# w_out by two-by-two blocks with seven products in an encoder block on one core

## The chip, the cores and the metric

The kernel runs on one core of a Trainium2 chip. The metric is the device time of one execution in microseconds (us), the median of several runs. The engines are named as in the profile: PE (TensorE matmul), PEld (its weight load), DVE (VectorE), ACT (ScalarE), POOL (GpSimd), SP (SyncE, which issues most transfers).

## What is computed

One layer of an encoder on a stream of 16 meta tokens and 1024 frames, width 1024, all float32: a half-step SwiGLU feed-forward, a mixing part (window attention and gated linear attention, GLA), a second half-step feed-forward, a final norm. The part that matters here, from the reference:

```python
    mixed = (jax.nn.sigmoid(gate_a) * (ya @ w_branch_att[l])
             + jax.nn.sigmoid(gate_b) * (yb @ w_branch_gla[l]))
    h = h + mixed @ w_out[l]
    h = h + 0.5 * swiglu(rmsnorm(h, ffn2_norm[l]), ffn2_w_gate[l], ffn2_w_up[l], ffn2_w_down[l])
```

`mixed` is 1024 wide, `w_out` is 1024 x 1024. Only the 1024 frames go through this part.

## The kernel before

**Number format.** Each float32 matrix is cut into a high and a low half in fp32r (`hi = cast(x)` on ACT, `lo = x - hi` on DVE), and each product of two 128-wide tiles is three matmuls: hi x hi, hi x lo, lo x hi. Tokens lie along the free axis, features along the 128 partitions, so a matmul of 512 columns is 128 features by 512 tokens.

**The feed-forwards** already multiply by blocks: `Seven` splits weights and tokens two by two and makes seven block products of the eight, with sums of weight blocks (S1 to S4) and of token blocks (T1 to T4). Their order and accumulators are in `PRODUCTS`; `Group.sums` makes S1 to S4 and `halves` makes the cuts. Their matmuls are line 464, their weight cuts lines 229 and 230, the weight sums line 447, the reading of a bank in the down projection line 344.

**The branch products** (`branch_units`): `ya @ w_branch_att` was multiplied by its gate and stored in `gates`; then `yb @ w_branch_gla` runs in 16 units (8 feature tiles m, 2 token halves). `load_b` fetches both gates' tiles, `ev_b` multiplies the bank (`br`) by the sigmoid (line 1584), adds the stored half (line 1585), and splits the result into `mx_` (lines 101, 102), tiles `mh` and `ml`.

**w_out** comes next: for each token half c and each of the 8 feature tiles m, a weight tile of 128 columns is fetched (512 KB) and cut (lines 125, 126), so each weight is fetched and cut twice. One bank `wo` takes 24 matmuls (8 k x 3, lines 96 to 98). DVE adds the residual `hm`, which was fetched from `h_dram` (line 1646), ACT squares it, and POOL, near the end DVE, adds the squares into `acc` (line 1657). `scales_total` sums `acc` over features with four small matmuls (`tot`) and takes the root, `scales_spread` turns the result into rows, and `rescale` (line 1623) makes the normed tokens, which are cut to be the second feed-forward's operands.

**After it** the feed-forward's last two feature tiles (`HEADS`) are done plainly, eight products' worth at a time (`plain`, banks `pg` and `pu`); then the token sums and the seven-product loop (`gate_ups`, `down`).

**Order of the work.** A scheduler orders each engine's instructions by priority and readiness, except inside `manual_schedule`, where the engines named keep the order in which the code is written. w_out stands outside such a piece. A tile pool (`tile_pool`) gives its memory back when it is closed; whoever takes the same place next waits until its last reader is done. [...]

```python
    for c in range(2):
        ...
        for m in range(KT):
            wh, wl = ktiles(wt.cut(wt.raw(cols_view(w_out, m * P))))
            hm = ub[c][m] = block("hm")
            nc.sync.dma_start(out=hm, in_=h_dram[m, :, c * HALF:(c + 1) * HALF])
            ps = bank("wo")
            cols = slice(c * HALF, (c + 1) * HALF)
            mm(ps, wh, wl, [t[:, cols] for t in mx_[0]], [t[:, cols] for t in mx_[1]])
            ...
            nc.vector.tensor_add(hm, ps, hm)
```

Of the kernel before, what the change touches and what calls it, by code (L numbers as in the profile page):

```python
# [8 lines left out]
F32 = mybir.dt.float32  # L9
# [8 lines left out]
P = 128  # L18
# [17 lines left out]
def hybrid_kernel(  # L36
# [25 lines left out]
    def ttile(name, dt=F32, n=512):  # L62
        return tmp.tile([P, TW], dt, tag="t", name=name)[:, 0:n]
# [1463 lines left out]
    def out_gate(i, chunks):  # L1527

        for c0, n in chunks:
            a, g = ttile("a"), ttile("g")  # L1530
            nc.sync.dma_start(out=a, in_=gr_dram[i, :, c0:c0 + n])
            nc.scalar.activation(g, a, AF.Sigmoid)
            nc.vector.tensor_mul(a, a, g)
            pt = bank("ot")
            o = heads[i // 2].o[i % 2]
            for t in range(4):
                nc.tensor.transpose(pt[:, t * P:(t + 1) * P], o[:, c0 + t * P:c0 + (t + 1) * P], ident)
            nc.vector.scalar_tensor_tensor(a, pt, vec[:, GO:GO + 1], a, op0=ALU.mult, op1=ALU.mult)
            split(yb[0][i][:, c0:c0 + n], yb[1][i][:, c0:c0 + n], a)
# [25 lines left out]
        fill.pop(0)()  # L1565
    for i in range(4):
        out_gate(i, CH_FR[1:2])
    right.close()


    mx_ = [[atile(f"m{hl}{i}", F32R) for i in range(KT)] for hl in "hl"]

    def load_b(m, c0, n):
        l = []
        for i in (8 + m, m):
            g = gtile("gl") if i < 8 else ttile("gl")
            nc.sync.dma_start(out=g[:, 0:n], in_=gates[i, :, c0:c0 + n])
            l.append(g)
        return l

    def ev_b(ps, m, c0, n, l):
        gb, a = l[0][:, 0:n], l[1][:, 0:n]
        nc.scalar.activation(gb, gb, AF.Sigmoid)
        nc.vector.tensor_mul(gb, ps[:, 0:n], gb)
# [4 lines left out]
    for u in units[0][0:2] + units[1][0:2] + units[0][2:4] + units[1][2:4] + units[2] + units[3]:  # L1589
        u()  # L1590
    gla.close()

    HALF = 512
    right = ctx.enter_context(ExitStack())
    t_a = right.enter_context(tc.tile_pool(name="ta", bufs=8, side="right"))
    blk = right.enter_context(tc.tile_pool(name="blk", bufs=17, side="right"))
    pools = [t_a, None, blk, None, w_main]  # L1600
    h2_dram = dram.tile([2, KT, P, HALF], F32, name="h2_dram")

    def scales_total(acc):
        ps = bank("tot")
# [17 lines left out]
        u = ub[c][m]  # L1622
        nc.vector.scalar_tensor_tensor(u, u, vec[:, G2 + m:G2 + m + 1], accs[c], op0=ALU.mult, op1=ALU.mult)

    def acc2(kind, which, turn):
        return bank(f"p{kind}")

    ffn2 = Seven("f2", HALF, acc2, pools, ffn2_w_gate, ffn2_w_up, ffn2_w_down)
    tops, block = ffn2.tops, ffn2.block
    ub = [[None] * KT, [None] * KT]  # L1630
    accs = []
    for c in range(2):
        acc = ttile(f"acc{c}")
        accs.append(acc)
        for m in range(KT):
            wh, wl = ktiles(wt.cut(wt.raw(cols_view(w_out, m * P))))
            hm = ub[c][m] = block("hm")
            nc.sync.dma_start(out=hm, in_=h_dram[m, :, c * HALF:(c + 1) * HALF])
            ps = bank("wo")
            cols = slice(c * HALF, (c + 1) * HALF)  # L1640
            mm(ps, wh, wl, [t[:, cols] for t in mx_[0]], [t[:, cols] for t in mx_[1]])
            if c == 1 and m == 0:
                first_dg = scales_total(accs[0])
            if c == 1 and m == 1:
                scales_spread(accs[0], first_dg)
            nc.vector.tensor_add(hm, ps, hm)
            if c == 1 and m >= 1:
                for k in (range(2) if m == 1 else [m] if m < KT else []):
                    rescale(k, 0)
                    tops["B11" if k < 4 else "B21"][k % 4] = ffn2.halves(ffn2.operand(True, "tb"), ub[0][k])  # L1650
            nc.sync.dma_start(out=h2_dram[c, m], in_=hm)
            if m == 0:
                nc.scalar.activation(acc, hm, AF.Square)
            else:
                sq = ttile("sq")
                nc.scalar.activation(sq, hm, AF.Square)
                (nc.vector if m >= KT - 2 else nc.gpsimd).tensor_add(acc, acc, sq)
# [6 lines left out]
    ffn2.w_ext = f2.enter_context(tc.tile_pool(name="wext2", bufs=2))  # L1664
    ffn2.s_pool = f2.enter_context(tc.tile_pool(name="sums", bufs=4))
    ffn2.ring = [w_main] * 6 + [ffn2.w_ext] * 2


    heads = [[ffn2.plain_weights(cols_view(w, f * P)) for w in (ffn2_w_gate, ffn2_w_up)] for f in HEADS]
    out_c = [[None] * 2 for _ in range(2)]  # L1670

    def plain(f, c, between=()):
        ts = [tops["B11"] + tops["B21"], tops["B12"] + tops["B22"]][c]
        pss = []
        for i in range(2):
            ps = bank("pg" if i == 0 else "pu")
            pss.append(ps)
            mm(ps, *ktiles(heads[f][i]), [x[:, 0:HALF] for x in ts], [x[:, HALF:] for x in ts])
            if between:
                between[i]()  # L1680
        g = ttile("g0")
        nc.scalar.activation(g, pss[0], AF.Silu)
        out_c[f][c] = block("m0")
        nc.vector.tensor_mul(out_c[f][c], pss[1], g)

    state = {}

    def second():
        state["dg"] = scales_total(accs[1])

    def third():
        scales_spread(accs[1], state["dg"])
        for m in range(KT):
            rescale(m, 1)
            tops["B12" if m < 4 else "B22"][m % 4] = ffn2.halves(ffn2.operand(False, "tb"), ub[1][m])
# [98 lines left out]
```

## Time and profile before

| what | value |
|---|---|
| median of 3 runs | 1999.52 us (1994.55 to 1999.86) |
| span of the profiled execution | 1994.6 us |
| granted TensorE clock, mean | 0.999 |
| PE busy | 1976.3 us, 99% |
| DVE, ACT, POOL busy | 1402.4, 897.2, 166.9 us |
| GLA branch products on PE | about 1210 to 1253 us |
| w_out on PE | about 1253 to 1342 us |
| plain gate/up and start of the loop | from 1342 us |

The profiled execution's own time is its span, within 0.1 us of the fastest of the three runs and 4.9 us below their median. In the profile's rows a group is line, engine, operation, out<-in, shape and count, then busy us and mean ns of one, then idle time before it and what ended it. In the time line a row is start, length, engine, line and operation.

### The profile page before, as it was taken

How to read it: one execution, taken by the hardware profiler on the slowest of the kernel's cores; microseconds unless marked ns; L12 is line 12 of the kernel's file. 1: busy time of each engine (PE TensorE's matmuls, PEld its weight loads, DVE VectorE, ACT ScalarE, POOL GpSimd, SP SyncE). 2: the span in 40 equal slices, each digit the busy share in tenths (PEclk: the TensorE clock that was granted, in tenths of full speed). 3: DMA queues.
4: the chain of work that ended last, by engine and by line, in shares of the span. 5: the costliest groups of instructions: out<-in, count | busy, mean ns of one | idle time of the engine just before them, and what ended most of it. 6: DMA issues, size and time to landing. Idle time of an engine off the chain costs nothing. (4 is left out here: it accounts for less than half of the span.)

```text
span 1994.6 us, 31746 instructions
## 1 busy us (share of the span) xinstructions
PE 1976.3 (99%) x11964; PEld 1755.8 (88%) x11964; DVE 1402.4 (70%) x2455; ACT 897.2 (45%) x1756; POOL 166.9 (8%) x196
## 2 busy tenths in 40 slices
PE   8999999999999999999999999999999999999998
PEld 8999999999999988888888778888888888888887
DVE  6976776677678785476466568568767766767886
ACT  5544444444322254465366545345444544442225
POOL 1000000001222000004100000110000000022220
PEclk9999999999999999999999999999999999999999
DMA  6343454348875333355212647742434543589722
GB/s 214 108 150 126 146 180 137 118 150 322 271 283 194 96 124 109 110 184 176 53 54 70 205 151 218 249 139 79 160 127 137 187 142 127 190 300 328 282 102 85
DMA packets 279721, 328.23 MB, mean 165 GB/s; under 512 B 25734, under 2 KB 191360, under 8 KB 279568
## 3 DMA queue, kind: packets, MB, share of 16 engines
q1 hardware_dynamic: 263936, 272.20, 41.5%
q10 hardware_dynamic: 15280, 53.89, 7.5%
q8 instruction: 94, 1.54, 0.3%
q14 instruction: 59, 0.48, 0.1%
q0 software_dynamic: 352, 0.11, 0.1%
HBM read 213.26 MB, written 112.88 MB: 164 GB/s over the span
## 5 line engine op out<-in xcount | busy, mean ns | idle before, releaser
L464 PE MATMUL pb<-tt,wop 128*128 128x260 f32 (+1 forms) x2280 | 393.0, 326 | 0.0
L464 PEld LDWEIGHTS pb<-tt,wop 128*128 128x128 f32 x2280 | 339.7, 188 | 35.5
L229 ACT CAST wop<-s 128x512 fp32r<-128x512 f32 x268 | 166.1, 621 | 236.9 <-PE pb L464 102.9
L230 DVE TENSOR_TENSOR wop<-s,wop 128x512 fp32r<-128x512 f32 x268 | 187.9, 704 | 114.8 <-ACT wop L229 114.3
L464 PE MATMUL pb<-tm,wop 128*128 128x260 f32 (+1 forms) x1440 | 233.7, 318 | 0.0
L229 ACT CAST wop<-raw 128x512 fp32r<-128x512 f32 x201 | 124.8, 621 | 225.4 <-PE pb L464 114.7
L464 PEld LDWEIGHTS pb<-tm,wop 128*128 128x128 f32 x1440 | 207.0, 188 | 18.7
L230 DVE TENSOR_TENSOR wop<-raw,wop 128x512 fp32r<-128x512 f32 x201 | 140.0, 697 | 34.3 <-ACT wop L229 34.2
L464 PE MATMUL pd<-tt,wop 128*128 128x260 f32 (+1 forms) x792 | 138.2, 327 | 0.0
L464 PEld LDWEIGHTS pd<-tt,wop 128*128 128x128 f32 x792 | 118.8, 188 | 13.1
L447 POOL TENSOR_TENSOR s<-raw 128x512 f32<-128x512 f32 x28 | 37.4, 1336 | 1025.0 <-DVE wop L230 538.8
L344 DVE SCALAR_TENSOR_TENSOR h<-pb,h 128x520 f32<-128x520 f32 (+1 forms) x136 | 94.0, 693 | 37.3 <-PE pb L464 35.4
L464 PE MATMUL pd<-tm,wop 128*128 128x260 f32 (+1 forms) x720 | 118.8, 319 | 0.0
L464 PE MATMUL pb<-tb,wop 128*128 128x260 f32 (+1 forms) x696 | 115.3, 319 | 0.7 <-DVE m L752 0.7
L464 PE MATMUL pd<-tb,wop 128*128 128x260 f32 (+1 forms) x696 | 115.1, 319 | 0.0
L464 PE MATMUL pa<-tb,wop 128*128 128x260 f32 (+1 forms) x696 | 115.0, 318 | 0.0
L464 PEld LDWEIGHTS pd<-tm,wop 128*128 128x128 f32 x720 | 104.2, 188 | 9.4
L464 PEld LDWEIGHTS pb<-tb,wop 128*128 128x128 f32 x696 | 100.9, 188 | 10.2 <-ACT vec L87 0.8
L464 PEld LDWEIGHTS pa<-tb,wop 128*128 128x128 f32 x696 | 100.7, 188 | 9.4
L464 PEld LDWEIGHTS pd<-tb,wop 128*128 128x128 f32 x696 | 100.7, 188 | 9.4
L447 DVE TENSOR_TENSOR s<-raw 128x512 f32<-128x512 f32 x92 | 63.3, 688 | 54.5 <-DMA raw<-in_ffn_w_up 50.6
L96 PE MATMUL pj<-uh,whi 128*128 128x512 f32 (+2 forms) x256 | 91.5, 357 | 0.0
(417 smaller groups left out, 3880.2 us busy)
## 6 DMA issues: line engine op xcount, KB each, us to landing
tm<-f1mid ACTq DMA_DIRECT2D x49, 520.0 KB, 5.4
tm<-f2mid ACTq DMA_DIRECT2D x49, 512.0 KB, 4.6
raw<-in_ffn_w_gate SPq DMA_DIRECT2D x42, 512.0 KB, 3.9
raw<-in_ffn_w_up SPq DMA_DIRECT2D x42, 512.0 KB, 3.9
raw<-in_ffn_w_down SPq DMA_DIRECT2D x80, 256.0 KB, 5.1
f1mid<-kh SPq DMA_DIRECT2D x63, 260.0 KB, 2.7
f1mid<-kl SPq DMA_DIRECT2D x63, 260.0 KB, 2.8
f2mid<-kh SPq DMA_DIRECT2D x63, 256.0 KB, 2.8
```

The costliest lines, as they stand in the source:

```text
L96: nc.tensor.matmul(ps, wh[k], xh[k], start=(k == 0), stop=False)
L229: nc.scalar.copy(x[:, 0:n], src)
L230: nc.vector.tensor_sub(x[:, n:2 * n], src, x[:, 0:n].bitcast(F32))
L344: nc.vector.scalar_tensor_tensor(hm, ps, 0.5, hm, op0=ALU.mult, op1=ALU.add)
L447: (eng.tensor_add if add else eng.tensor_sub)(a[s], a[x], a[y])
L464: nc.tensor.matmul(ps, y, z[:, s0:s0 + sn], start=(first and k == 0 and at == 0), stop=(at == 2 and k == len(cols) - 1), skip_group_check= ...
```

## The change

w_out becomes seven block products as in the feed-forward. Weights are four 512 x 512 blocks: A11 and A12 for the first 512 output features (first and second 512 input features), A21 and A22 for the rest. Tokens are B11, B21 (input features 0 to 511 and 512 to 1023 of the first token half), B12, B22 (second half). `ev_b` keeps the mixed tokens as raw float32 (`raw11`, `mixed`) and cuts B11, B21 and B22 (not B12) into operands `mx`. Each of the seven steps runs over four k-tiles; for each of the 28 pairs (i, k) four banks take three matmuls each. Weights are cut by `weights_of`, three pairs ahead; four kinds of bank group are used: b (steps 0, 2, 3, 4, one group, accumulating), a (step 1), d (steps 5, 6).

The residual is added in the reading of a bank: `started` adds the bank to the fetched residual, `finished` with a bank adds a second bank to it, `finished` without one stores the sum and squares it. A bank group b is read after step 0 (in the middle of step 1), after step 2, after step 3 and after step 4.

Weight sums and T4 go to POOL, T1 to T3 to DVE; the low halves of T1's cuts, of the `HEADS` weights (`head_weights`) and of five of the eight first operands (`first_tops`) go to POOL. The whole piece up to the end of the first `plain` is inside `manual_schedule` for ACT, DVE and PE; POOL and SP are ordered by the scheduler. `plain` runs gate and up side by side over k, with the second half's total (`second`) after k = 4. A21 and A22 lie in a pool (`ta`) that is opened when the branch's operands (`yb`) are done with.

```diff
+    raw11 = mix.enter_context(tc.tile_pool(name="raw11", bufs=4))
+    yb_pool = ybs.enter_context(tc.tile_pool(name="yb", bufs=8))
...
+    STEPS = (("b", "A11", "B11"), ("a", "A12", "B21"), ("b", "S2", "T2"), ("b", "S3", "T3"), ("b", "A22", "T4"),
+             ("d", "S1", "T1"), ("d", "S4", "B22"))
+    def weights_of(i, k):
+        w, a = ffn2.ring_tile("wop"), wa[STEPS[i][1], k]
+        cut_w[i, k] = w
+        nc.scalar.copy(w[:, 0:WB], a)
+        nc.vector.tensor_sub(w[:, WB:], a, w[:, 0:WB].bitcast(F32))
+    def cut_operand(name, k, src, eng=None):
+        x = wtop[name, k] = opd("mx")
+        nc.scalar.copy(x[:, 0:HALF], src)
+        (eng or nc.vector).tensor_sub(x[:, HALF:2 * HALF], src, x[:, 0:HALF].bitcast(F32))
...
-        split(mx_[0][m][:, c0:c0 + n], mx_[1][m][:, c0:c0 + n], a)
+        name, k = f"B{m // 4 + 1}{c0 // HALF + 1}", m % 4
+        mixed[name, k] = a
+        if name != "B12":
+            cut_operand(name, k, a)
...
+    ybs.close()
+    t_a = right.enter_context(tc.tile_pool(name="ta", bufs=8, side="right"))
...
+    def weight_sums(k):
+        s1 = wa["S1", k] = s1_tiles[k // 2][:, (k % 2) * WB:(k % 2 + 1) * WB]
+        nc.gpsimd.tensor_add(s1, wa["A21", k], wa["A22", k])
+        wa["S3", k] = wa["A21", k]
+        nc.gpsimd.tensor_sub(wa["S3", k], wa["A11", k], wa["A21", k])
+        wa["S2", k] = wa["A11", k]
+        nc.gpsimd.tensor_sub(wa["S2", k], s1, wa["A11", k])
+    def t_sum(name, k):
+        x, y = {"T1": ("B12", "B11"), "T3": ("B22", "B12"), "T2": ("B22", "T1"), "T4": ("B21", "T2")}[name]
+        to = {"T1": "B11", "T3": "B12", "T2": "B22", "T4": "B21"}[name]
+        (nc.gpsimd if name == "T4" else nc.vector).tensor_sub(mixed[to, k], mixed[x, k], mixed[y, k])
...
+    for k in range(4):
+        work[0, k] += [lambda k=k: weight_sums(k)]
+        work[3, k] += [lambda k=k: last_weight_sum(k)]
...
+    for n, (i, k) in enumerate(steps):
+        kind, _, name = STEPS[i]
+        if n + AHEAD < len(steps):
+            weights_of(*steps[n + AHEAD])
+        fresh = kind not in banks
+        if fresh:
+            banks[kind] = [bank(f"p{kind}") for _ in range(4)]
+        w, x = cut_w.pop((i, k)), wtop[name, k]
+        for j in range(4):
+            wh, wl = w[:, j * P:(j + 1) * P], w[:, WB + j * P:WB + (j + 1) * P]
+            for at, (y, z) in enumerate(((wh, x[:, 0:HALF]), (wh, x[:, HALF:2 * HALF]), (wl, x[:, 0:HALF]))):
+                nc.tensor.matmul(banks[kind][j], y, z, start=(fresh and k == 0 and at == 0), stop=(at == 2 and k == 3),
+                                 skip_group_check=True)
+        for go in work[i, k]:
+            go()
+        while waiting and (i, k) in ((1, 0), (2, 0)):
+            waiting.pop(0)()
...
+                elif i == 2:
+                    started(1, j, ps)
...
+    plain(0, 0, {0: lambda: head_weights(1, 0, (w_main, w_main)), 4: second, 5: lambda: head_weights(1, 1, (w_main, w_main)), 7: third})
```

What stands in the engines' own orders. On POOL, before, the only work of the w_out stretch are the additions of squares, up to the gate/up loop's weight sums (`acc` is the running sum, `sq` one tile's squares):

```order
L1657 TENSOR_TENSOR acc0_14128<-acc0_14128,sq_14200 128x512
L1657 TENSOR_TENSOR acc0_14128<-acc0_14128,sq_14238 128x512
L1657 TENSOR_TENSOR acc0_14128<-acc0_14128,sq_14276 128x512
L1657 TENSOR_TENSOR acc0_14128<-acc0_14128,sq_14314 128x512
L1657 TENSOR_TENSOR acc0_14128<-acc0_14128,sq_14352 128x512
```

On POOL, now, from the same place (line 1702 makes S1, 1704 S3, 1706 S2, 1710 S4, 1715 T4; `wa2` holds A21 or A22, `wa11` A11, `wa12` A12):

```order
L1715 TENSOR_TENSOR mixed_13949<-mixed_13949,mixed_13995 128x512
L1702 TENSOR_TENSOR s1_14159<-wa2_14147 128x512
L1702 TENSOR_TENSOR s1_14159<-wa2_14150 128x512
L1704 TENSOR_TENSOR wa2_14147<-wa11_13743,wa2_14147 128x512
L1704 TENSOR_TENSOR wa2_14150<-wa11_13743,wa2_14150 128x512
L1706 TENSOR_TENSOR wa11_13743<-s1_14159,wa11_13743 128x512 x2
L1702 TENSOR_TENSOR s1_14160<-wa2_14153 128x512
L1715 TENSOR_TENSOR mixed_13972<-mixed_13972,mixed_14018 128x512
L1704 TENSOR_TENSOR wa2_14153<-wa11_13744,wa2_14153 128x512
L1702 TENSOR_TENSOR s1_14160<-wa2_14156 128x512
L1706 TENSOR_TENSOR wa11_13744<-s1_14160,wa11_13744 128x512
L1704 TENSOR_TENSOR wa2_14156<-wa11_13744,wa2_14156 128x512
```

Thirteen sums stand here where additions of squares stood; S4 of the first k and S2 of the last come next, then three more S4 and two T4 before the first addition of squares.

On DVE, before, at the end of the branch and the start of w_out (`ml` is a low half of mixed tokens, `wlo` of a weight tile, `hm` the residual):

```order
L102 TENSOR_TENSOR ml6_13740<-gl_14076,mh6_13732 128x512
L1584 TENSOR_TENSOR gl_14096<-br_14100,gl_14096 128x512
L1585 TENSOR_TENSOR gl_14098<-gl_14098,gl_14096 128x512
L126 TENSOR_TENSOR wlo_14206<-raw_14203,whi_14205 128x1024
L102 TENSOR_TENSOR ml7_13741<-gl_14098,mh7_13733 128x512
L126 TENSOR_TENSOR wlo_14244<-raw_14241,whi_14243 128x1024
L1646 TENSOR_TENSOR hm_14135<-wo_14137,hm_14135 128x512
L1646 TENSOR_TENSOR hm_14171<-wo_14173,hm_14171 128x512
```

On DVE, now, from the first cut of a T2 operand (line 1615) over weight cuts (1602) and token sums (1715) to the first reading of a bank (1683):

```order
L1615 TENSOR_TENSOR mx_14206<-mixed_13995,mx_14206 128x512
L1602 TENSOR_TENSOR wop_14212<-wa12_13751,wop_14212 128x512
L1715 TENSOR_TENSOR r11_13788<-mixed_13883,r11_13788 128x512
L1715 TENSOR_TENSOR mixed_13883<-mixed_14018,mixed_13883 128x512
L1715 TENSOR_TENSOR mixed_14018<-mixed_14018,r11_13788 128x512
L1602 TENSOR_TENSOR wop_14233<-wa12_13753,wop_14233 128x512
L1615 TENSOR_TENSOR mx_14248<-mixed_14018,mx_14248 128x512
L1602 TENSOR_TENSOR wop_14254<-wa12_13755,wop_14254 128x512
L1715 TENSOR_TENSOR r11_13817<-mixed_13903,r11_13817 128x512
L1715 TENSOR_TENSOR mixed_13903<-mixed_14099,mixed_13903 128x512
L1715 TENSOR_TENSOR mixed_14099<-mixed_14099,r11_13817 128x512
L1683 TENSOR_TENSOR hm_14276<-pb_14169,hm_14276 128x512
```

Where the first reading of a bank followed the last weight cut directly, eleven cuts and sums of two SBUF tiles now stand ahead of it.

More of the change, by code (lines that the diff above doesn't have):

```diff
@@ L1567, in hybrid_kernel @@
         out_gate(i, CH_FR[1:2])
+    gla.close()
     right.close()
-    mx_ = [[atile(f"m{hl}{i}", F32R) for i in range(KT)] for hl in "hl"]
-    def load_b(m, c0, n):
[L1574 to L1579, printed above, removed]
+    HALF = 512
+    right = ctx.enter_context(ExitStack())
+    blk = right.enter_context(tc.tile_pool(name="blk", bufs=17, side="right"))
@@ new lines, in hybrid_kernel, with acc2 @@
+    w_ext = right.enter_context(tc.tile_pool(name="wext2", bufs=2, side="right"))
+    s_pool = right.enter_context(tc.tile_pool(name="sums2", bufs=4, side="right"))
+    h2_dram = dram.tile([2, KT, P, HALF], F32, name="h2_dram")
+    def acc2(kind, which, turn):
+        return bank(f"p{kind}")
+    ffn2 = Seven("f2", HALF, acc2, [None, None, blk, s_pool, w_ext], ffn2_w_gate, ffn2_w_up, ffn2_w_down)
+    tops, block = ffn2.tops, ffn2.block
+    wa, wtop = {}, {}
+    a11 = [w_ext.tile([P, 1024], F32, tag="w", name="wa11", align_bytes=128) for _ in range(2)]
@@ new lines, in hybrid_kernel @@
+    for k in range(4):
+        wa["A11", k] = a11[k // 2][:, (k % 2) * WB:(k % 2 + 1) * WB]
+        nc.sync.dma_start(out=wa["A11", k], in_=w_out[k * P:(k + 1) * P, 0:WB])
+    for k in range(4):
+        wa["A12", k] = s_pool.tile([P, WB], F32, tag="s", name="wa12")
+        nc.sync.dma_start(out=wa["A12", k], in_=w_out[(4 + k) * P:(5 + k) * P, 0:WB])
+    cut_w = {}
+    def weights_of(i, k):
[3 more added lines that the diff above has]
+        nc.vector.tensor_sub(w[:, WB:], a, w[:, 0:WB].bitcast(F32))
@@ L1581, in ev_b @@
+    def load_b(m, c0, n):
+        gb = ttile("gl")
+        nc.sync.dma_start(out=gb, in_=gates[8 + m, :, c0:c0 + n])
+        a = raw11.tile([P, HALF], F32, tag="r", name="r11") if (m < 4 and c0 == 0) else block("mixed")
+        nc.sync.dma_start(out=a, in_=gates[m, :, c0:c0 + n])
+        return gb, a
     def ev_b(ps, m, c0, n, l):
-        gb, a = l[0][:, 0:n], l[1][:, 0:n]
+        gb, a = l
         nc.scalar.activation(gb, gb, AF.Sigmoid)
@@ L1623, in rescale @@
         nc.vector.scalar_tensor_tensor(u, u, vec[:, G2 + m:G2 + m + 1], accs[c], op0=ALU.mult, op1=ALU.mult)
[L1625 to L1629, printed above, removed]
     ub = [[None] * KT, [None] * KT]
[L1631 to L1645, printed above, removed]
-            nc.vector.tensor_add(hm, ps, hm)
[L1647 to L1657, printed above, removed]
@@ new lines, in hybrid_kernel, with head_weights @@
+    HEADS = [NF - LAST + f for f in range(LAST)]
+    heads = [[None] * 2 for _ in HEADS]
+    def head_weights(f, i, pools):
+        raw = ffn2.plain_raw(cols_view((ffn2_w_gate, ffn2_w_up)[i], HEADS[f] * P))
+        hi, lo = [p.tile([P, 1024], F32R, tag="w", name=n, align_bytes=128) for p, n in zip(pools, ("whi", "wlo"))]
+        heads[f][i] = hi, lo
+        nc.scalar.copy(hi, raw)
+        nc.gpsimd.tensor_sub(lo, raw, hi.bitcast(F32))
+    work[4, 1].append(lambda: head_weights(0, 0, (w_ext, w_ext)))
@@ new lines, in hybrid_kernel, with plain @@
+    out_c = [[None] * 2 for _ in range(2)]
+    def plain(f, c, between={}):
+        ts = [tops["B11"] + tops["B21"], tops["B12"] + tops["B22"]][c]
+        pss, ws = [bank(x) for x in ("pg", "pu")], [ktiles(heads[f][i]) for i in range(2)]
+        for k in range(KT):
+            for ps, (wh, wl) in zip(pss, ws):
+                xh, xl = ts[k][:, 0:HALF], ts[k][:, HALF:]
+                nc.tensor.matmul(ps, wh[k], xh, start=(k == 0), stop=False)
+                nc.tensor.matmul(ps, wh[k], xl, start=False, stop=False)
+                nc.tensor.matmul(ps, wl[k], xh, start=False, stop=(k == KT - 1))
+            if k in between:
+                between[k]()
+        g = ttile("g0")
+        nc.scalar.activation(g, pss[0], AF.Silu)
+        out_c[f][c] = block("m0")
+        nc.vector.tensor_mul(out_c[f][c], pss[1], g)
@@ L1658, in hybrid_kernel, with second, third @@
+    def second():
+        state["dg"] = scales_total(accs[1])
+    def third():
+        scales_spread(accs[1], state["dg"])
+    first_tops(6)
+    first_tops(7)
+    plain(0, 0, {0: lambda: head_weights(1, 0, (w_main, w_main)), 4: second, 5: lambda: head_weights(1, 1, (w_main, w_main)), 7: third})
+    manual.__exit__(None, None, None)
+    plain(1, 0)
+    mix.close()
     acts.close()
@@ L1663, in hybrid_kernel @@
     nc.gpsimd.memset(shift, 0.0)
[L1664 to L1695, printed above, removed]
+    ffn2.ring, ffn2.slot = [w_main] * 6 + [w_ext] * 2, 0
+    for m in range(KT):
+        rescale(m, 1)
+        tops["B12" if m < 4 else "B22"][m % 4] = ffn2.halves(ffn2.operand(False, "tb"), ub[1][m])
     def others(n, k):
```

106 lines of the change are left out of this document (93 added, 13 removed).

## Prediction

> **What bounds the kernel now.** I read the page's head first, then the chain of waits, then the stretch of w_out by windows, and last the instructions of DVE and POOL where the two overlap. The head of the page:
>
> ```profile
> span 1994.6 us, 31746 instructions
> PE 1976.3 (99%) x11964; PEld 1755.8 (88%) x11964; DVE 1402.4 (70%) x2455; ACT 897.2 (45%) x1756; POOL 166.9 (8%) x196
> ```
>
> PE is busy for 99% of the span, so what PE does not have to do is time saved, and what PE has to wait for is time lost, one for one. The chain of waits gives PE's pace and the windows the stretch that the change touches (columns: length, then busy us and count of PE, PEld, DVE, ACT, POOL, then clock, DMA share, GB/s):
>
> ```profile
> 1389.68 2.72 PE pa L464 x12
> ...
> 1253.20:1341.90 88.70, 88.70 (x399) 73.56 (x398) 49.34 (x59) 33.92 (x46) 17.97 (x10) 1.00 0.59 190
> ```
>
> Twelve matmuls of 512 columns take 2.72 us, 0.2267 each. In the 88.7 us of w_out PE never stops, the granted clock is 1.00, and DVE has 39 us to spare: every other engine is hidden here. The groups of w_out by shape:
>
> ```profile
> L96 PE MATMUL wo<-mh,whi 128*128 128x512 f32 x128 | 50.0, 391 | 0.0
> L98 PE MATMUL wo<-mh,wlo 128*128 128x512 f32 x128 | 49.8, 389 | 0.0
> L97 PE MATMUL wo<-ml,whi 128*128 128x512 f32 x128 | 49.8, 389 | 0.0
> ```
>
> Each has no idle time before it (last column).
>
> **PE's saving.** 384 matmuls (3 x 128) become 7 products x 4 k-tiles x 4 banks x 3 = 336, of the same shape. 48 x 0.2267 = 10.9 us less. The pace holds only if operands come in time.
>
> **What DVE and POOL get instead.** POOL has ten instructions in the old stretch. It now gets 4 weight sums and 1 token sum for each of 4 k, 4 cuts of T1, 4 cuts of gate/up weights, 6 sums of squares and 5 cuts of the next stage's operands. Their price by shape, and the price of DVE's usual instruction (five in a row):
>
> ```profile
> L447 POOL TENSOR_TENSOR s<-raw 128x512 f32<-128x512 f32 x28 | 37.4, 1336 | 1025.0 <-DVE wop L230 538.8 <-DMA tm<-f1mid 435.2 <-DMA raw<-in_ffn_w_down 31.8
> L1657 POOL TENSOR_TENSOR acc<-acc,sq 128x512 f32<-128x512 f32 x10 | 18.0, 1797 | 176.9 <-DMA raw<-in_w_out 129.5 <-ACT sq L1656 47.5
> L126 POOL TENSOR_TENSOR wlo<-raw,whi 128x1024 fp32r<-128x1024 f32 x2 | 4.8, 2401 | 1.4 <-ACT whi L125 0.9 <-issue 0.5
> ...
> 1372.90 3.10 DVE L230 TENSOR_TENSOR tt<-hm,tt 128x512 fp32r<-128x512 f32 x5
> ```
>
> The same addition on POOL is 1.34 us in the down projection but 1.80 in w_out. DVE's is 0.69 alone and (3.10 - 0.69) / 4 = 0.60 in a row. Why POOL's price varies is seen where the two engines overlap (time line: start, length):
>
> ```profile
> 579.23 1.30 POOL L447 TENSOR_TENSOR s<-raw,raw 128x512 f32<-128x512 f32 x1 [1.58 <-DVE wop L230]
> 579.93 1.15 DVE L414 TENSOR_TENSOR h<-h,old 128x520 f32<-128x520 f32 x1
> ...
> 616.81 0.69 DVE L414 TENSOR_TENSOR h<-h,old 128x520 f32<-128x520 f32 x1
> 617.02 1.64 POOL L447 TENSOR_TENSOR s<-s,raw 128x512 f32<-128x512 f32 x1 [1.90 <-issue]
> 617.42 1.31 DVE L344 SCALAR_TENSOR_TENSOR h<-pd,h 128x520 f32<-128x520 f32 x2
> ```
>
> At 579.93 a DVE addition of two SBUF tiles starts during a POOL one and lasts 1.15 instead of 0.69: it ends 0.55 after POOL's end at 580.53. At 617.02 it is the other way: POOL ends 1.16 after DVE's end at 617.50. The two readings from PSUM at 617.42 (one SBUF input) run inside POOL's time unharmed, 1.31 for two. So a two-input DVE instruction and a two-input POOL instruction exclude each other, and when they take turns a pair costs 1.16 + 0.55 = 1.71 us. [...]
>
> **The term that decides: the first three products.** Call T the start of the first product. The order shows, on DVE, from T to the first reading of the third product's banks, 41 instructions: 32 with two SBUF inputs (operand and weight cuts, token sums) and 9 with PSUM input. POOL has 22 in that piece, of which 14 must be done, since the fourteenth is the weight sum S2 of k = 3. Products one, three, four and five accumulate in the same four banks, so each of the later ones waits for DVE to read them. PE's own time for three products is 3 x 4 x 2.72 = 32.6 us; the first bank is due to be read at T + 30.6 (a bank is finished 3 x 0.68 ahead of the end).
> Lower end: all excluded time in a row with no loss, readings hidden: 32 x 0.60 + 14 x 1.16 = 35.4, a stall of 4.8. Upper end: all 22 of POOL and all 41 of DVE one after the other, 24.6 + 25.5 = 50.1, a stall of 19.5. Between them by turns: POOL's loads are issued when the branch's last matmul frees their place, and land some 4 us later.
>
> ```profile
> gl<-gates SPq DMA_DIRECT2D x28, 256.0 KB, 3.8
> raw<-in_w_out SPq DMA_DIRECT2D x16, 512.0 KB, 4.8
> ...
> 1257.19 0.69 DVE L1584 TENSOR_TENSOR gl<-br,gl 128x512 f32<-128x512 f32 x1
> 1260.26 1.22 DVE L126 TENSOR_TENSOR wlo<-raw,whi 128x1024 fp32r<-128x1024 f32 x1
> ```
>
> (Column after the size: us to landing. DVE is late by 4 to 8 us at this place already now: T is the left edge of the window above, 1253.2.) From T + 4 twelve two-input DVE instructions stand ahead of the first bank reading: 12 x 1.71 = 20.5. Then 4 readings x 0.60 and the third product's first cut 0.7: T + 27.6, where PE is due at 21.8. Stall 5.8. Then 15 more two-input and 4 reading instructions with 9 or 10 of POOL: 9 x 1.71 + 6 x 0.60 + 4 x 0.60 = 21.4, plus 0.7 for the reading itself, T + 49.7, where PE is due at 27.6 + 10.9 = 38.5. Stall 11.2. Together 17.0, less up to 2.4 where the readings run inside POOL's time: **16 us**, ends 4.8 and 19.5. I take the turns because who wins is seen at 481 us and 1318 us:
>
> ```profile
> 481.39 0.70 DVE L230 TENSOR_TENSOR tm<-g,tm 128x520 fp32r<-128x520 f32 x1
> 481.48 1.77 POOL L447 TENSOR_TENSOR s<-raw,s 128x512 f32<-128x512 f32 x1 [1.16 <-issue]
> 482.01 1.79 DVE L278 TENSOR_TENSOR tm<-u,g 128x520 f32<-128x520 f32 x1
> ...
> 1317.71 0.68 DVE L230 TENSOR_TENSOR tb<-hm,tb 128x512 fp32r<-128x512 f32 x1
> 1318.00 3.28 POOL L1657 TENSOR_TENSOR acc<-acc,sq 128x512 f32<-128x512 f32 x1 [5.81 <-ACT sq L1656]
> 1318.32 1.22 DVE L126 TENSOR_TENSOR wlo<-raw,whi 128x1024 fp32r<-128x1024 f32 x1
> 1319.45 0.68 DVE L230 TENSOR_TENSOR tb<-hm,tb 128x512 fp32r<-128x512 f32 x1
> 1320.05 2.45 DVE L1623 SCALAR_TENSOR_TENSOR hm<-hm,vec,acc 128x512 f32<-128x512 f32 x2
> ```
>
> At 482 POOL got ahead of a DVE instruction that already stood ready; at 1318 it lost twice (3.28 us) and won the third time. Turns fit better than either always winning.
>
> **The rest.** From the fourth product to the end of the first gate/up tile PE has 4 x 10.9 + 10.9 = 54.4 us; POOL 12 x 1.34 + 4 x 2.40 = 25.7, DVE 43 two-input x 0.62 = 26.7: 52 of exclusive time, just enough on average. But the sums of squares of the second half now end inside that tile and their total is a PE instruction at its k = 4, some 6.8 us after the last product; four readings (2.4), the last square and four additions (about 3) and a POOL cut of 2.40 between them make 8 to 9. I put 3, ends 0 and 6. At the branch's end token sums and weight cuts enter DVE's list while four operand cuts leave it: 0.6, ends 0 and 1.4. Costed at nothing: w_out is fetched once instead of twice, 16 issues of 512 KB become 16 of 256 KB, hidden as before (DMA share 0.59); ACT's 28 half-size weight cuts and 28 operand cuts are covered by its idle half (33.92 of 88.70), but ACT stands in order behind DVE and shares its delay, which is in the turns.
>
> **Sum.** -10.9 + 16 + 3 + 0.6 = +8.7 us. Against the profiled execution, 1994.6, that is 2003.3; its span lies 4.9 us below the median of the three runs, 1999.5, which is what I add it to: **2008 us**, +0.4%. From the ends, -10.9 + 4.8 = -6 (1993) and -10.9 + 19.5 + 6 + 1.4 = +16 (2016).
>
> **Rivals.**
> [...] If DVE's chain mostly wins, as twice at 1318, DVE runs ahead, its bank readings come on time, and POOL's 14 sums fall into DVE's waits. The stall is then 5 to 8, the rest 2 to 3: -10.9 + 10 = -1, 1998.5. [...] Chance 0.25, nearly all of it within 0.3%.
> *The saving comes through.* The place is the bank reading after the third product: as long as DVE is there by T + 30.6, PE does not stop. For it: PE lost nothing in 88.7 us that held 49 of DVE and 18 of POOL. Against: that is 67 in 88.7, and now some 40 are due in 30.6. It decides if a weight sum costs DVE under about 0.4 us instead of 1.16. Then -10.9 + 1 = 1989.5. Chance 0.17.
> *The tail is late too.* If the gate/up cuts on POOL stretch as at 1318 (3.28 for 1.34), their 2.40 become 4 to 5 and the first gate/up tiles wait 6 us more: 2015 to 2018. Chance 0.08.
> *PE does not get its pace*, because four weight tiles alternate on one moving tile. The present products alternate in the same way at 2.72 for twelve. Time then near 1999; chance 0.03.
>
> **The numbers.** Forecast 0.47, rivals 0.25, 0.17, 0.08, 0.03. About 0.3% (6 us) is what a measurement of this kernel can tell from no change. Slower: 0.47 + 0.08 = 0.55; same: 0.22 + 0.03 = 0.25; faster: 0.17 + 0.03 = 0.20. The range 1993 to 2017 runs from the sum's lower end to its upper and the third rival's middle, and leaves out the second rival and half of the third, 0.2. The forecast alone: 2003 to 2013.
>
> **What would show it.** Right: PE waits for `pb` behind DVE before the third and the fourth product, 5 and 10 us; POOL's additions in that stretch near 1.7 us, DVE's cuts up to 1.8; 336 matmuls at 0.2267; a wait of 2 to 3 us ahead of the second `tot`. Wrong: POOL's additions at 1.3 with DVE's at 0.6 side by side, or PE idle below 5 us in the seven products.

## The result and the profile after

The changed kernel takes 2015.78 us (median of 4 runs, 2013.48 to 2019.58), the kernel before beside it 1998.63: ratio 1.0092, 95% interval 1.0075 to 1.0109. It is slower by 17 us, where 8.7 were forecast. The profiled execution took 2014.35 us with a span of 2012.6, 18.0 more than the span before. The page's head, after:

```profile
span 2012.6 us, 31743 instructions
PE 1973.4 (98%) x11916; PEld 1749.0 (87%) x11916; DVE 1444.6 (72%) x2494; ACT 903.2 (45%) x1780; POOL 214.2 (11%) x224
```

PE has its 48 matmuls less (11964 to 11916), DVE 42 us more and POOL 47. The stretch of the prediction's window, taken 8 us longer (columns as in the prediction: busy us and count of PE, PEld, DVE, ACT, POOL, then clock, DMA share, GB/s):

```profile
1253.20:1350.00 96.80, 83.36 (x353) 67.42 (x352) 83.69 (x93) 36.40 (x63) 50.30 (x32) 0.93 0.29 95
```

PE, which never stopped here, now idles 13.4 us, DVE has 13 us left instead of 39, and the granted clock is 0.93 instead of 1.00. What PE waited for between 1190 and 1440 us is in the view of waits (waiting line, releasing line: us in total, times, longest); before, the same view is empty:

```profile
PE pb L1775 <- DVE hm L1683: 7.3, 1, 7.3
PE pb L1775 <- DVE wop L1602: 3.6, 2, 2.0
PE pb L1775 <- ACT mx L1614: 2.6, 1, 2.6
PE br L98 <- DVE wlo L126: 2.5, 1, 2.5
PE tot L1657 <- DVE acc L1698: 2.4, 1, 2.4
PE br L96 <- ACT ybh L101: 1.8, 2, 1.4
```

The first three rows are the first three products, the fourth and the last the branch, the fifth the second total. And the clock, by windows at the waits ahead of the third and the fourth product and just after the total:

```profile
1284.00:1288.00 4.00, 2.40 (x7) 1.58 (x7) 4.00 (x6) 0.87 (x2) 4.00 (x4) 0.55 0.00 0
1288.00:1292.00 4.00, 4.00 (x12) 3.19 (x11) 3.96 (x3) 0.00 (x0) 4.00 (x3) 0.60 0.00 0
...
1304.00:1308.00 4.00, 0.00 (x0) 0.00 (x0) 4.00 (x6) 3.25 (x7) 1.08 (x1) 0.61 0.46 135
...
1368.00:1372.00 4.00, 4.00 (x17) 3.21 (x16) 2.60 (x3) 0.91 (x1) 4.00 (x2) 0.78 0.05 14
```

From 1288 to 1292 PE is busy all the time and starts 12 matmuls, where 4.00 / 0.2267 is 17.6: after a wait of 2.6 us PE ran at half clock for a while, with a granted clock of 0.50 from 1284.41 to 1291.23.

All of it can be counted in the trace by the distance between one 512-column matmul and the next. What the distances over 0.5 us have above 0.2267 adds up to the waits (handover included, and less the 2.3 us that the small matmuls of the totals already take before the change); the excess of the smaller distances is slow running. The table has these sums from the end of the transpositions to 1450 us for every kernel, in us, and the stage length from the last transposition of the gated branch heads (line 1539 in the changed kernel) to the last matmul of the down projection, which leaves out what earlier stages did. Each ratio is to the kernel before as measured beside that kernel (medians 1996.16 to 1998.63), so times of different rows are compared by their ratios.

| kernel | branch | first products | total and after | slow running (half clock, us) | stage | time, ratio to before [interval] |
|---|---|---|---|---|---|---|
| before | 0 | 0 | 0 | 0.4 (0) | 777.0 | 1998.63 |
| after | 5.4 | 14.8 | 2.6 | 6.4 (17.1) | 795.2 | 2015.78, 1.0092 [1.0075, 1.0109] |
| e1_sums_on_dve | 4.9 | 9.5 | 2.6 | 6.2 (17.1) | 789.1 | 2009.41, 1.0064 [1.0052, 1.0077] |
| e2_no_sums | 5.2 | 0 | 3.6 | 4.6 (6.8) | 779.4 | 1998.13, 1.0006 [0.9997, 1.0015] |
| e3_sums_unread | 4.3 | 14.1 | 2.6 | 6.5 (17.1) | 793.4 | 2013.43, 1.0087 [1.0073, 1.0101] |
| e4_total_later | 3.9 | 12.6 | 8.7 | 9.3 (20.5) | 800.5 | 2024.02, 1.0136 [1.0122, 1.0150] |
| e5_branch_loads | 3.5 | 12.5 | 3.7 | 7.4 (13.7) | 793.0 | 2013.08, 1.0082 [1.0070, 1.0094] |
| e6_dummies | 4.9 | 14.4 | 1.1 | 3.5 (13.7) | 803.8 | 2026.88, 1.0160 [1.0145, 1.0175] |
| e7_sums_early | 11.4 | 2.4 | 2.6 | 4.2 (13.7) | 786.5 | 2006.61, 1.0053 [1.0041, 1.0065] |
| e8_combined | 3.9 | 3.1 | 2.6 | 3.9 (6.8) | 779.4 | 1999.55, 1.0020 [1.0011, 1.0029] |
| e9_loads_squares | 1.2 | 3.9 | 2.7 | 4.9 (10.2) | 778.6 | 1996.88, 1.0005 [0.9996, 1.0013] |
| e10_tail | 1.2 | 3.6 | 2.8 | 4.2 (6.8) | 777.4 | 1997.59, 1.0008 [0.9999, 1.0016] |
| e11_dummies_total | 4.8 | 13.4 | 1.1 | 7.4 (17.1) | 795.3 | 2016.87, 1.0099 [1.0083, 1.0114] |
| e12_ahead | 1.2 | 3.5 | 3.6 | 1.4 (0) | 775.2 | 1995.76, 0.9997 [0.9988, 1.0006] |

For the changed kernel: -10.9 + 5.4 + 14.8 + 2.6 + (6.4 - 0.4) = 17.9, and the stage is 18.2 longer. The account closes, and the same sum gives the stage of every other row within 0.4 us (with 13.8 us of added matmuls in e6_dummies and 2.5 in e11_dummies_total). In e7_sums_early 9.2 of the branch's 11.4 are at the head of the first product. The waits are of one profiled execution each; how far two of them differ is seen in e4_total_later and e11_dummies_total, whose code for the branch and the first products is that of the changed kernel: 3.9 and 4.8 in the branch, 12.6 and 13.4 in the products, for 5.4 and 14.8.

### The profile page after: what moved, and what is told of

It reads as the page before. It is cut to its first block, busy times and chain, and to the rows that moved or that the text cites. A ratio compares the mean times of both kernels' runs of the same rounds, so it can differ in the third digit from the quotient of the medians.

```text
span 2012.6 us, 31743 instructions
## 1 busy us (share of the span) xinstructions
PE 1973.4 (98%) x11916; PEld 1749.0 (87%) x11916; DVE 1444.6 (72%) x2494; ACT 903.2 (45%) x1780; POOL 214.2 (11%) x224
## 4 chain that ended last, share of the span: by engine, by line
PE 86%; DVE 6%; DMA 3%; issue 2%; ACT 2%; POOL 0%; SPq 0%; DVEq 0%; ACTq 0%; POOLq 0%
PE pb L464 37%; PE pd L464 18%; PE pa L464 9%; PE pj L96 2%; PE pj L97 2%; PE pj L98 2%; PE pd L851 1%; PE pj L939 1%; PE pj L940 1%; PE pj L941 1%; PE pb L1775 1%; DMA gl<-gates 1%; DVE mx L1615 1%; PE tp L1327 1%; PE po L1343 1%
## 5 line engine op out<-in xcount | busy, mean ns | idle before, releaser
L464 PEld LDWEIGHTS pb<-tb,wop 128*128 128x128 f32 x696 | 100.9, 188 | 10.2 <-ACT vec L87 0.8
```

What stands on the lines that cost most here:

```text
L464: nc.tensor.matmul(ps, y, z[:, s0:s0 + sn], start=(first and k == 0 and at == 0), stop=(at == 2 and k == len(cols) - 1), skip_group_check= ...
```

## The experiments

The theory behind the prediction: POOL's sums and DVE's instructions with two SBUF inputs exclude each other (1.71 us a pair in the rows of before), DVE falls behind, and the reading of the banks comes late. Rivals: DVE's list is too long by itself; or the operands come late because POOL's sums do.

**e1_sums_on_dve: the same sums on DVE, two (product, k) pairs later.**

```diff
-        nc.gpsimd.tensor_add(s1, wa["A21", k], wa["A22", k])
+        nc.vector.tensor_add(s1, wa["A21", k], wa["A22", k])
...
-        work[0, k] += [lambda k=k: weight_sums(k)]
+        work[(2 + k) // 4, (2 + k) % 4] += [lambda k=k: weight_sums(k)]
```

> The same sums, all on DVE: the 16 weight sums and the four T4 sums leave POOL, and the sums of a k-tile are issued two (product, k) pairs later. Theory 'taking turns' (POOL's sums and DVE's two-input instructions exclude each other, so each POOL sum costs DVE about 1.1 us): DVE pays 0.60 to 0.69 for a sum instead of about 1.1 of waiting; the waits of the first three products fall from 14.8 us to 5 to 8, the half-clock time with them, DVE's cuts in that stretch last 0.6 to 0.7; about 2005 us. Rival 'DVE's list is too long by itself': 16 to 20 more instructions of 0.6 lengthen the list by 10 us, the waits grow to about 24, about 2025 us.

Measured: 2009.41, 6 us less; the products' waits are 9.5, between the two expectations (5 to 8, and 24). With POOL silent DVE's sums last 0.69 (groups between 1250 and 1320 us: busy, mean ns of one | idle before):

```profile
L1706 DVE TENSOR_TENSOR wa<-s,wa 128x512 f32<-128x512 f32 x4 | 2.8, 692 | 0.1
...
L1715 DVE TENSOR_TENSOR mixed<-mixed,r 128x512 f32<-128x512 f32 x4 | 2.8, 689 | 0.1
```

So the sums cost less on DVE, where they also come two pairs later; the edit does not part the two. But 20 sums more on DVE do not fit either: part of the wait is the length of its list.

**e2_no_sums and e3_sums_unread: no sums, and sums for nobody.** Both compute less: the products read unsummed blocks. In the first the 16 weight sums and the four T4 sums are left out; in the second POOL makes as many, on the same loads, into a place nobody reads.

```diff
-        nc.gpsimd.tensor_add(s1, wa["A21", k], wa["A22", k])
-        wa["S3", k] = wa["A21", k]
-        nc.gpsimd.tensor_sub(wa["S3", k], wa["A11", k], wa["A21", k])
...
+        for s, a in (("S1", "A21"), ("S3", "A21"), ("S2", "A11")):
+            wa[s, k] = wa[a, k]
```

> Leaves out the 16 weight sums and the four T4 sums: the products read unsummed blocks in their place, all else stays. 'Taking turns': with POOL empty DVE's two-input instructions are 0.6 to 0.7 us, the first three products' 14.8 us of waits go to 0 to 2 and the half-clock time there (about 6 us at half loss) with them: 1996 to 2000 us; what stays above the sum (before minus 10.9) is the branch's 5.4 and the total's 2.6. Rival 'DVE's list is too long by itself' (41 instructions and its turns with ACT): the waits stay above 8, 2008 or more. Rival 'operands come late' (the chain load, POOL sums, cut): goes as 'taking turns'.

> As without sums (the products read unsummed blocks), but POOL does the same 20 additions on the same loads into a place that nobody reads. 'Taking turns': DVE's cuts stay at 1.6 to 1.8 us beside POOL and most of the 14.8 us of waits stays, since it does not matter who reads the sums: 2008 to 2014 us. Rival 'operands come late' (products wait because a sum on POOL ends late): nobody waits for POOL now, the waits go as without sums, 1996 to 2000 us.

Measured: 1998.13 and 2013.43. Without sums the products' waits are 0, with sums for nobody 14.1. That takes "operands come late" out: nobody waited for a sum in e3_sums_unread. It also takes out the list by itself at 41 instructions: DVE's own list is the same in both. DVE's token sums in e3_sums_unread and in e2_no_sums, and POOL's sums in the former (groups between 1250 and 1320 us, one fence for each kernel):

```profile
L1703 POOL TENSOR_TENSOR s<-wa,wa 128x512 f32<-128x512 f32 x4 | 7.0, 1754 | 0.0
...
L1719 DVE TENSOR_TENSOR mixed<-mixed,r 128x512 f32<-128x512 f32 x4 | 5.7, 1416 | 0.1
```

```profile
L1712 DVE TENSOR_TENSOR mixed<-mixed,r 128x512 f32<-128x512 f32 x4 | 2.8, 690 | 0.1
...
L1682 DVE TENSOR_TENSOR hm<-pb,hm 128x512 f32<-128x512 f32 x16 | 10.7, 688 | 4.4 <-PE pb L1772 4.4
```

The same DVE instruction takes 1.42 with POOL at work and 0.69 without. And e2_no_sums says something the forecast had not seen: even with this stall gone altogether the change only breaks even (1.0006), because 5.2 of the branch, 3.6 of the tail and 4.2 of half clock are more than the 10.9.

**e4_total_later: the second total three k later.**

```diff
-    plain(0, 0, {..., 4: second, 5: lambda: head_weights(1, 1, (w_main, w_main)), 7: third})
+    plain(0, 0, {..., 5: lambda: head_weights(1, 1, (w_main, w_main)), 7: second})
+    plain(1, 0, {4: third})
```

> Only the place of the totals of squares moves: the second total from k = 4 to k = 7 of the first gate/up tile, the work after it from k = 7 there to k = 4 of the next tile. If the 2.6 us of PE at the second total are its own and the half clock of 3.4 us behind it comes from that wait: 2.6 + 1.7 = 4.3 less, about 2011.5 us, granted clock 1.0 after 1360. Rival 'the delay is the list's, it only moves': the next gate/up tile waits for its normalised operands instead, no change, 2014 to 2016 us.

Measured: 2024.02, 8 us more, which neither side expected. The wait at the total is gone, and PE waits for the gate/up operands at the same moment and for the next stage's later on:

```profile
PE pb L464 <- DVE wop L230: 4.5, 1, 4.5
...
PE pg L1812 <- ACT tb L1739: 2.0, 1, 2.0
...
PE pg L1813 <- POOL tb L1740: 0.9, 1, 0.9
```

I read the total's 2.6 us as a sign that DVE's list is late there; put off, the scalings of the second half are later by more.

**e5_branch_loads: the loads of A11 and A12, and the first two weight cuts of w_out, behind the branch's own.**

```diff
+    loads = tc.manual_schedule(engines={nc.sync.engine})
+    loads.__enter__()
+    for u in units[2] + units[3][0:1]:
+        u()
+    for k in range(4):
+        wa["A11", k] = a11[k // 2][:, (k % 2) * WB:(k % 2 + 1) * WB]
+        nc.sync.dma_start(out=wa["A11", k], in_=w_out[k * P:(k + 1) * P, 0:WB])
...
+    loads.__exit__(None, None, None)
```

> Only the order of loads in the branch changes: the eight loads of A11 and A12 are issued behind the branch's own loads (the first three weights, the first gate of the last) instead of between the loads of its operands. Theory 'the new loads are in the way' (a<-gr_dram issued 2.3 to 4.6 us later than before the change, gl<-gates late, DVE idle behind them): the branch's waits of 5.4 us go to 0 to 1; the later waits stay: 2009 to 2011 us. Rival 'DVE's list carries the branch's delay' (weight cut behind token additions): the waits at the branch stay at 4 to 5, 2014 to 2016 us; or the 5 us reappear in the first products' waits.

Measured: 2013.08, ratio 1.0082 against 1.0092: the intervals overlap. The branch's waits are 3.5, as neither side expected, and not far below the 3.9 to 5.4 of the seven profiles with the branch unaltered. The edit does more than the expectation says: with the first unit of the last branch weight it also puts that weight's cut on DVE ahead of the first weight cuts of w_out. The branch's waits are of two kinds. The first (2.7 of 5.4 in the changed kernel, 1.7 to 3.6 in the seven profiles) is for `ybh`, which waits for the loads `a` (ACT stands 3.8 and 2.7 us for two of them). In the changed kernel SP's queue at this place is

```profile
1206.96 0.42 SPq L1595 DMA_DIRECT2D wa<-in_w_out  x1
1209.94 0.32 SPq L1533 DMA_DIRECT2D a<-gr_dram  x1
...
1219.34 0.32 SPq L1533 DMA_DIRECT2D a<-gr_dram  x1
...
1220.18 0.43 SPq L117 DMA_DIRECT2D raw<-in_w_branch_gla  x1
```

where the first `a` load was issued at 1207.65 before. With the loads of w_out behind, this kind is 1.2 to 1.7, in e5_branch_loads and in the four later kernels that have that order. The second kind (2.8, in the seven profiles 1.2 to 2.8) is for the low half of the branch's last weight. Its load came later than before (issued at 1220.18, before at 1200.5), but that is not what PE waits for: ACT has cast it at 1238.41, and on DVE its cut stands 12 us further on, behind sixteen instructions, two of them weight cuts of w_out:

```profile
1237.38 1.03 ACT L125 CAST whi<-raw 128x1024 fp32r<-128x1024 f32 x1
...
1250.42 1.22 DVE L126 TENSOR_TENSOR wlo<-raw,whi 128x1024 fp32r<-128x1024 f32 x1
```

In e5_branch_loads the cut follows its cast at once and the wait for `wlo` is gone, but the weight itself now comes behind the gate loads (issued at 1236.30), and PE waits 1.6 us for its cast on ACT. e9_loads_squares below takes that away.

**e6_dummies and e11_dummies_total: matmuls by zeros where PE waits.**

```diff
+        for _ in range({(2, 0): 12, (2, 1): 8, (3, 0): 30}.get((i, k), 0)):
+            nc.tensor.matmul(banks["a"][3], zdum, wtop["B21", 3][:, 0:HALF], start=(i == 3), stop=(i == 3), ...)
...
+            if k == 4 and (f, c) == (0, 0):
+                for _ in range(11):
+                    nc.tensor.matmul(pss[0], zdum, ts[k][:, 0:HALF], start=False, stop=False)
```

The second kernel has only the last three lines.

> 61 added matmuls by a tile of zeros (12 and 8 before the first two k of the third product, 30 before the fourth, 11 before the second total), placed where PE waits, so that PE is busy there; nothing else changes. Theory 'a wait of some us halves the clock for one to two periods of 3.4 us afterwards' (about 6 us lost): clock 1.0 after each of the three places, 4 to 6 us less, 2010 to 2012 us. Rival 'the slow matmuls are slow because operands come just in time': the granted clock stays as it is or rises without gain, 2014 to 2018 us.

> The changed kernel with only the 11 matmuls by zeros ahead of the second total (11 x 0.2267 = 2.5 us, into the 2.6 us in which PE waits there). If the wait is what halves the clock afterwards: the wait and the half clock of 3.4 us behind it are gone, the time falls by about 1.7 us, 2013 to 2015 us. If the clock halves for another reason: half clock stays at 1366, time unchanged or up.

Measured: 2026.88 and 2016.87. As times the theory's expectations failed in both; the second kernel's time is unchanged, as its other side has it. In e6_dummies the 30 matmuls before the fourth product write a bank that DVE has yet to read, wait for that reading themselves and push the product back:

```profile
PE pa L1777 <- DVE hm L1692: 12.1, 1, 12.1
```

The clock went as the theory has it wherever the wait was really filled: at the third product of e6_dummies no half clock until 1293, and none after the second total in either kernel. Windows of e11_dummies_total there (0.79 and 0.78 without the added matmuls):

```profile
1362.00:1366.00 4.00, 3.97 (x18) 2.98 (x17) 3.90 (x6) 2.34 (x4) 4.00 (x4) 1.00 0.70 259
1366.00:1370.00 4.00, 4.00 (x23) 3.21 (x22) 3.23 (x5) 1.78 (x4) 0.53 (x2) 1.00 0.01 3
```

The gain of 1.7 us is not seen in the time: half clock elsewhere was longer in this execution (17.1 us in all, as without), and the interval is some 6 us wide. In e2_no_sums (granted clock 1.00 from 1320 to 1400) and e5_branch_loads no half clock follows the total either, with nothing added, so the two kernels alone do not show that PE's wait brings it on; the count over all traces in the last section shows which waits it followed. What one filled wait is worth in time is not shown.

**e7_sums_early and e8_combined.** Sums on DVE, eight of the token sums inside the branch, S3 (as A22 - S2), S4 and T4 a product later; e8_combined has the load order of e5_branch_loads as well.

```diff
+    for k in range(4):
+        t_sum("T1", k)
+    for k in range(2):
+        t_sum("T3", k)
+        t_sum("T2", k)
...
+        nc.vector.tensor_sub(wa["S3", k], wa["A22", k], wa["S2", k])
```

> The sums all on DVE as in the first experiment, but eight of the twelve token sums are made inside the branch, S3 (as A22 - S2) and T4 one product later. Theory: what holds the first three products is how many two-input instructions lie between the branch and the reading of the third product's banks; 8 sums (4.8 us) are taken out and 4 of S3 put off, so the 9.2 us of waits there fall to 0 to 3 and the half clock behind them goes: 1998 to 2002 us. Rival 'the list is held by the turns between ACT and DVE (cast, cut, cast)': the waits stay above 6, 2006 or more.

> As the kernel with the sums early, and A11's and A12's loads behind the branch's own. If both reasons hold the gains add: before minus 10.9 plus the total's 2.6 and its half clock 1.7 plus at most 3: 1990 to 1994 us, the first version below the kernel before. If the branch's 5 us only move into the products: as the kernel with the sums early.

Measured: 2006.61 and 1999.55; 4.6 and 5.6 us above the upper ends of what was expected. In e7_sums_early the products' waits fell from 9.5 to 2.4, as expected, but 8.6 us came up at the head of the first product, which waits for a weight cut that DVE makes only after the token sums (view of waits):

```profile
PE pb L1784 <- DVE wop L1602: 8.6, 1, 8.6
```

With the order of e5_branch_loads (e8_combined) that wait is gone and the gains add up: 7 us less than e7_sums_early, and a stage 15.8 us shorter than in the changed kernel.

**e9_loads_squares, e10_tail, e12_ahead: the rest one by one.** The first loads the branch's last weight earlier and puts the first squares on DVE; the second adds each square in the tail right after its bank is read, with the total at k = 5; the third takes seven DVE instructions out of the list before the fourth product.

```diff
+    raws[6] = wt.raw(cols_view(w_branch_gla, 6 * P, 2 * P, 4))
-            (nc.vector if squared[c] > 4 else nc.gpsimd).tensor_add(accs[c], accs[c], sq)
+            nc.vector.tensor_add(accs[c], accs[c], sq)
...
+                    if j:
+                        finished(1, j - 1)
...
-        if (i, k) == (2, 1):
+        if (i, k) == (3, 1):
```

> As the combined kernel, with its two waits of 2.6 and 2.7 us taken away: the last branch weight is loaded before three of the branch's gate loads instead of after them, and the first squares of each half are added on DVE, so that POOL has nothing to add while DVE cuts the operands of the fourth product (POOL's three additions lasted 6.45 us there, two DVE cuts beside them 3.48 instead of 1.28). If that is the cause: no wait at the branch's last weight and none before the fourth product, with its half clock 1.7: 5 to 7 us less than the combined kernel, 1992 to 1995 us. If it is DVE's list by itself: three additions more on DVE, no gain or 1 us more, 1998 to 2001 us.

> As the kernel before it in this list, and in the last product each square is added right after the next bank is read instead of after all four, with the second total at k = 5 of the first gate/up tile instead of k = 4. If the 2.6 us at the total are the row of four readings and four additions: 2.6 less and the half clock of 1.7 with it, so 3 to 4 us less than the kernel before it. If the delay is that of DVE's list of scalings and cuts behind it: it moves to the gate/up operands, 0 to 1 us.

> As the kernel with the rearranged tail, and DVE's list ahead of the fourth product is made shorter: the weight cuts of the first two products are put five pairs ahead instead of three, two cuts of T2 are made inside the branch, and the squares of the first four output tiles come a product later. If the wait of 3.6 us before the fourth product is the number of DVE instructions between the branch and there: three additions, two operand cuts and two weight cuts less, 7 x 0.60 = 4.2 us, so the wait goes and the half clock of 1.7 with it: about 1992 us, 2 per mille below the kernel before. If DVE has no idle time in the branch to take them (it waits for nothing there either): the wait stays at 2 or more or comes back in the branch, 1995 to 1998 us.

Measured: 1996.88, 1997.59 and 1995.76. e9_loads_squares: the time lies between its two expectations. The branch is down to 1.2, since the wait for its last weight is gone. But the wait before the fourth product, 3.1 with POOL's three additions, is 3.9 without them: they were not its cause. e10_tail: in the view of waits the total's fell from 1.7 to 0.7 and came up as 1.1 before the next operands; the delay moved, as the second expectation has it. e12_ahead: the wait before the fourth product fell from 3.6 to 2.1, with 0.6 and 0.8 at its neighbours, so the sum is what it was (3.5), and the time is as the second expectation has it; but in these pieces the waits were followed by no half clock at all in the stretch (granted clock 1.00 from 1215 to 1350). Its stage is 775.2 against 777.0 before, but the time (0.9997, interval 0.9988 to 1.0006) cannot be told from the kernel before. What became of the 11 us of PE is in the windows from the branch on, first of e12_ahead (to 8 us behind the end of w_out), then of the kernel before (to the end of w_out):

```profile
1215.00:1350.00 135.00, 131.19 (x580) 106.75 (x577) 118.15 (x182) 64.70 (x109) 17.38 (x11) 1.00 0.52 173
```

```profile
1210.00:1341.00 131.00, 131.00 (x586) 108.59 (x585) 86.53 (x116) 59.34 (x86) 17.97 (x10) 1.00 0.64 204
```

DVE is busy for 118 of 135 us (110 of 127 up to the end of w_out), where it was for 86.5 of 131. Over the whole execution it is 1434.7 us against 1402.4: 32 us of DVE for 10.9 of PE.

## Why the prediction was right or wrong

- *PE's saving, -10.9*: right. 336 matmuls (192 of `pb`, 48 of `pa`, 96 of `pd`) at 0.2267 where operands are there and the clock is full.
- *The first three products, +16*: right in mechanism, 14.8 in size (12.6 to 14.8 in the three profiles that leave this part as it is). PE waited for `pb` before the third product (4.9 us in three pieces, forecast 5.8, with 2.2 more inside that product) and before the fourth (7.8 in two, forecast 11.2). That the sum agrees better than its parts is in part luck: POOL's first weight sum began at 1265.2, 4 us behind the branch's last matmul as worked out, but that matmul came at 1260.7 and not at T (1253.2), and the first product had begun inside the branch, at 1247.2. The order of POOL's and DVE's instructions by turns is in the time line of the changed kernel, DVE first, then POOL (start, length):

```profile
1289.35 1.76 DVE L1715 TENSOR_TENSOR r<-mixed,r 128x512 f32<-128x512 f32 x1
1291.15 1.67 DVE L1715 TENSOR_TENSOR mixed<-mixed 128x512 f32<-128x512 f32 x1
1292.85 1.67 DVE L1715 TENSOR_TENSOR mixed<-mixed,r 128x512 f32<-128x512 f32 x1
...
1288.84 1.72 POOL L1710 TENSOR_TENSOR wa<-wa,wa 128x512 f32<-128x512 f32 x1
1290.53 1.74 POOL L1715 TENSOR_TENSOR mixed<-mixed 128x512 f32<-128x512 f32 x1
1292.22 3.41 POOL L1710 TENSOR_TENSOR wa<-wa,wa 128x512 f32<-128x512 f32 x2
```

  In these rows each ends a fixed time after the other's end, DVE 0.55 us after POOL's (1291.11 after 1290.56) and POOL 1.16 after DVE's (1292.27), 1.7 us a pair as worked out.
- *The rest, +3*: right, 2.6, at the second total as named. In e4_total_later and e10_tail the wait only moved to the next operands, as it would if DVE's list is late there.
- *The branch's end, +0.6 (ends 0 and 1.4)*: this step failed. It measured 5.4 in the changed kernel's profile, and 3.9 to 5.2 in six others with the branch unaltered. Half of it (2.8) is DVE's list, where the step had looked, but the cut of the branch's last weight stands in it 12 us behind its cast; the step had counted instructions that enter and leave, not what is put behind them. The other half (2.7) is loads, which were costed at nothing, "hidden as before" by a DMA share of 0.59. That share was that of the w_out stretch; the loads are issued in the branch ahead of it, which was fuller. Its window before, and then after (DMA share and GB/s are the last two columns):

```profile
1200.00:1247.00 47.00, 47.00 (x217) 39.18 (x216) 39.07 (x62) 24.70 (x38) 0.00 (x0) 1.00 0.73 226
```

```profile
1200.00:1247.00 47.00, 44.95 (x204) 36.35 (x203) 33.78 (x54) 19.12 (x30) 0.00 (x0) 1.00 0.91 296
```

  With the branch's own loads and its last weight's cut ahead again the waits are 1.2 (e9_loads_squares). The share alone does not settle it: in e8_combined it is 0.66 and the waits are 3.9. The last 1.2 are waits for `ybh` too; why they stay is open.
- *The half clock*: this step failed too, a term that the sum did not have, 6.0 us. Every wait was priced at its own length. Nothing in the trace of before showed the price, since PE never waited in this part; the waits forecast would have been the reason to look for one.
- *The sum*: +8.7 forecast, +17.9 by the account above. Of the 9.2 between, the branch is 4.8 and the clock 6.0; the other terms give back 1.6. The time lies at the upper edge of the range, and inside the 2015 to 2018 of "The tail is late too", by luck: that rival looked for its 6 us in cuts at the tail, and neither of the two terms that failed was in it.
- *The rivals*: the first, in which DVE's chain mostly wins, and "The saving comes through" are out by the time line and by e2_no_sums beside e3_sums_unread. "The tail is late too" did not occur in size: the waits from the total on are 2.6. "PE does not get its pace" is out by the 0.2267 us of the first bullet.

## What to carry to other kernels

On a kernel whose PE is full, a product saved is worth its time only if the engines that prepare its operands have that time; count the two-input instructions of DVE and POOL as one resource, since beside POOL's additions a DVE instruction took 1.42 us here (e3_sums_unread) instead of 0.69 (e2_no_sums). A load or a cut that is moved or added is to be priced in the stage in which it is issued, by what stands behind it in the queue, and not in the stage that uses it. And waits of PE can cost more than their length: here 22.8 us of them went with 6.0 us more of slow running at half clock, a term that a forecast of stalls needs, while the 8.3 us of e12_ahead, in smaller pieces, were followed by no half clock.

## What the runs showed of the hardware that was not expected

After waits of a few us PE's granted clock was 0.5 for 3.4, 6.8 or 10.2 us (13.7 in e6_dummies): after the 2.6 us at the total 3.4, after 7.8 us before the fourth product 6.8 (more than half of it still inside the wait). The length of a wait alone does not tell: 1.7 us at the total in e9_loads_squares (view of waits) was followed by 6.8 us of half clock, while 2.8 us in the changed kernel's branch and 2.1 us in e12_ahead were followed by none.

What stood ahead of the half clock can be counted in the traces. In each of the 14 all changes of the clock lie on one grid of steps of 3.41 us, and the steps part by how much of one is empty, without a 512-column matmul (0.2267 us each, 0.4533 at half clock). Between 1204 and 1450 us there are 961 steps at full clock: the 32 with 2.10 us or more empty were all followed by half clock, the 929 with 2.06 or less were not. Of the 47 steps at half clock the 15 with 1.06 or more empty were followed by another, the 32 with 0.60 or less by full clock. So in these traces the position of a wait counted. In the changed kernel the steps with 2.87, 3.41 and 3.08 empty were followed by half clock, and the other steps at full clock have at most 1.8. There the 2.8 us of the branch fall on two steps, with 1.5 and 1.6 empty (first two rows), the 2.6 us at the total into one, with 3.1 empty (third row), and of the two waits only this one has a clock of 0.50 in the next step (fourth row; PE's busy time also holds small matmuls). In e12_ahead no step has more than 2.0 empty.

The rows of the changed kernel:

```profile
1246.86:1250.27 3.41, 2.34 (x10) 1.37 (x8) 2.31 (x4) 2.86 (x5) 0.00 (x0) 1.00 0.23 86
1250.27:1253.69 3.42, 1.99 (x9) 1.65 (x10) 3.42 (x6) 2.83 (x6) 0.00 (x0) 1.00 0.59 186
...
1362.92:1366.33 3.41, 1.31 (x10) 1.30 (x11) 3.08 (x5) 1.34 (x3) 0.06 (x1) 1.00 0.00 0
1366.33:1369.74 3.41, 3.41 (x10) 2.63 (x9) 2.82 (x3) 2.58 (x4) 3.08 (x2) 0.50 0.00 0
```

How matmuls of other shapes count is not shown.
